# A decoder layer on one core: four per-layer-embedding products between the MLP's last sums, in source order

## The chip, the cores and the metric

The kernel runs on one core of one Trainium2 chip. The metric is the device time of one execution in microseconds (us), lower is better. Before the change three runs gave 1787.39, 1788.55 and 1790.4 us, so the median is 1788.55 us.

## The reference

One hybrid decoder layer over 1024 tokens of width 1024, all in float32: a dilated attention and an RWKV-7 time mix side by side, merged by gates, then a squared-ReLU MLP with 4096 hidden units, then a gated per-layer input embedding ("ple"). The change touches the last two parts:

```python
        f = rmsnorm(h, ffn_pre_norm[i])
        f = jnp.square(jax.nn.relu(f @ w_ff_in[i])) @ w_ff_out[i]
        h = h + rmsnorm(f, ffn_post_norm[i])
        e = (p[i] @ w_ple[i]) * jax.nn.sigmoid(h @ w_ple_gate[i])
        h = h + rmsnorm(e, ple_post_norm[i])
```

`p @ w_ple` (256 to 1024 columns) does not depend on `h`. `h @ w_ple_gate` does, and needs the MLP's output complete for its tokens.

## The kernel before, in words

**How a product is made.** Float32 products are made of three passes over halves that TensorE takes at full rate: every operand is split into a high part (ScalarE copies it, rounded) and a low part (VectorE or GpSimd subtracts the high part), and `mm3` issues high x high, high x low and low x high for each 128 rows of the contraction. The lines L291, L293 and L295 are these three. All elementwise instructions are recorded at one line, L116, all DMA requests at L133 (the SP queue), transposes at L282.

**Stages.** Input projections with the RWKV chain beside them (to about 470 us), attention (to about 830), merges and the output projection, first MLP matrix and second MLP matrix interleaved (about 1000 to 1626). The second matrix is multiplied by a seven-product scheme over 16 groups of 256 hidden units; its sums stand in SBUF tiles `tot`. The last group is multiplied plainly: `ff2_last(i, c)` computes, for token tile `i` (128 tokens, 8 of them) and column half `c`, six matmuls of 512 columns, and VectorE adds the PSUM bank to the sum `acc(i, c)`. The banks of these products rotate over three tags (`bank()`: s1, s2, s3), so a product waits until the bank used three products earlier has been read.

**After the sums.** `finish(i)` is a chain spawned after `ff2_last(i, 1)`: two squares with a row sum on ScalarE, a sum, a root and a reciprocal, two VectorE products with the gain row `g3`, two additions of the residual `hl` (loaded from `h_scr`, 256 KB per half, one buffer per half; the second addition on GpSimd for `i > 0`). Then `put_T` transposes the tile on TensorE and splits it (ScalarE `wh`, VectorE `wl`). `gate_mm(i)` multiplies it with `w_ple_gate` (48 matmuls) and takes the sigmoid into `sg`; `e_mm(i)` computes `p @ w_ple` for the tile (12 matmuls in two banks), multiplies by `sg`, squares, normalises, adds the tile and stores it. `last_weights` loads and splits the eight 128-row pieces of `w_ple_gate` (512 KB each, "wpg": two ScalarE copies and two GpSimd subtractions each) through the two buffers of raw rows `wr`; `ple_weights` does it for `p` and `w_ple` ("pq", four pieces) at the first `gate_mm`.

**What sets the order.** A planner (`Order`) runs over the program with its own costs: chains (`spawn`) go first when their time has come, dense products fill TensorE between them, and the order in which it emits instructions is the order of TensorE's queue everywhere. For the other four queues this order is binding only inside `tc.manual_schedule`; that is so from the RWKV stage until `attention` leaves it (L968). From there to the end the framework's scheduler orders VectorE, ScalarE, GpSimd and SP by its own rules, and may move later loads and splits ahead. The planner's cost of a VectorE instruction (`Engine`, L95 to L100) gets a factor of 1.25 when it has two tensor operands outside PSUM and `shared` is set; `attention` clears `shared`.

Of the kernel before, what the change touches and what calls it, by code (L numbers as in the profile page):

```python
# [18 lines left out]
D = 1024  # L19
# [18 lines left out]
LEAD, SPARE, LAG = 0.4, 0.5, 0.4  # L38
TABLE = {AF.Exp: 0, AF.Sqrt: 1, AF.Sigmoid: 2, AF.Tanh: 2}
# [18 lines left out]


def in_psum(x):  # L60
    return "PSUM" in type(x.tensor if hasattr(x, "tensor") else x[:].tensor).__name__.upper()
# [20 lines left out]
class Engine:  # L82
# [8 lines left out]
    def __getattr__(self, name):  # L91
        f = getattr(self.eng, name)

        def call(*a, **kw):
            n = max(math.prod(x.shape[1:]) for x in a if hasattr(x, "shape"))  # L95
            o = self.order
            us = self.fixed + n * self.per * (1.8 if name == "transpose" else 1.0)
            if self.shared and sum(hasattr(x, "shape") and math.prod(x.shape[1:]) > 1 and not in_psum(x)
                                   for x in (*a[1:], *kw.values())) > 1:
                us *= 1.25  # L100
            if name == "activation" and a[2] in TABLE and self.table != TABLE[a[2]]:
                us += 1.3
# [12 lines left out]
            o.dep = max(self.end, o.dep)  # L115
            return f(*a, **kw)  # L116
# [128 lines left out]
def layer(ctx: ExitStack, tc: tile.TileContext, x, pT, wz, wup, w_out, wff1, w_ff2, w_ple, w_pleg,  # L245
# [901 lines left out]
    def combine(OT, OA, stat, sel):  # L1147
# [56 lines left out]
    in_turn = tc.manual_schedule(  # L1204
        engines={mybir.EngineType.DVE, mybir.EngineType.Activation, mybir.EngineType.Pool, mybir.EngineType.SP})
# [333 lines left out]
    def ff1(j):  # L1539
        def body(hi, lo):  # L1540
# [58 lines left out]
    def ff2_last(i, c):  # L1599
        def body():  # L1600
# [5 lines left out]
            if i + c == 0:  # L1606
                last_weights()
# [5 lines left out]

    def last_weights():
# [11 lines left out]
    def ple_weights():  # L1626
        pq = pieces(("BK", "UV", "BK2", "r", "k"), "pq", F32R)
        P["p"], P["w"] = (pq[0:2], pq[2:4]), (pq[4:6], pq[6:8])
        P["sg"] = [rtile([128, D], "sg", t) for t in ("Ep", "En", "a", "kk")]
        t = rtile([128, 2, D], "eg", "BT")  # L1630
        P["eg"] = [rtile([128, D], "eg", "px"), t[:, 0], t[:, 1]]
        P["g4"] = rtile([128, D], "g4", "MP")
        SY.dma_start(P["g4"], gains[4:5, :].to_broadcast([128, D]))
        for k in range(2):
            wsplit(pT[k * 128:(k + 1) * 128, :], [(P["p"][0][k], P["p"][1][k], full)])
            wsplit(w_ple[k * 128:(k + 1) * 128, :], [(P["w"][0][k], P["w"][1][k], full)])

    hT = {}

    def finish(i):  # L1640
        yield from wait(lambda: i == 0 or i - 1 in hT and (i < 2 or ("G", i - 2) in done))
        a = [acc(i, 0), acc(i, 1)]
        r = ss2(a, [rtile([128, 512], "j", "gst") for c in range(2)])
        for c in range(2):
            hl = rtile([128, 512], "hl", ("ex", "py")[c])
            SY.dma_start(hl, h_scr[i][:, halves[c]])
            V.scalar_tensor_tensor(a[c], a[c], r, P["g3"][:, halves[c]], op0=OP.mult, op1=OP.mult)
            (G if c and i else V).tensor_tensor(a[c], a[c], hl, OP.add)
        yield sch.until(sch.dep + 0.3)
        hi = wpool.tile([128, KT, 128], F32R, name="wh")  # L1650
# [4 lines left out]
    def gate_mm(i):  # L1655
        def body():
            if i == 0:
                ple_weights()
# [11 lines left out]
        sch.add(body, None, lambda: i in hT and sch.t >= hT[i][2])  # L1670

    def e_mm(i):
        def body():
            ts = slice(i * 128, i * 128 + 128)
            sg, eg = P["sg"][i % 4], P["eg"][i % 3]
            cols = halves if i < 7 else (halves[0], slice(512, 768), slice(768, 1024))
            sc = small.tile([128, 4], F32, name="sc")
            for n, c in enumerate(cols):
                ps = bank()[:, 0:c.stop - c.start]
                yield from mm3(ps, [(P["p"][0][k][:, ts], P["p"][1][k][:, ts], P["w"][0][k][:, c],  # L1680
                                     P["w"][1][k][:, c]) for k in range(2)])
                V.tensor_tensor(sg[:, c], sg[:, c], ps, OP.mult)
                S.activation(ps, sg[:, c], AF.Square, accum_out=sc[:, n:n + 1])
                (V if n else G).tensor_tensor(eg[:, c], sg[:, c], P["g4"][:, c], OP.mult)
                if n:
                    V.tensor_tensor(sc[:, n:n + 1], sc[:, n - 1:n], sc[:, n:n + 1], OP.add)
            r = rstd_of(sc[:, n:n + 1], "rs")
            for c in cols:
                V.scalar_tensor_tensor(sg[:, c], eg[:, c], r,
                                       acc(i, c.start // 512)[:, c.start % 512:(c.stop - 1) % 512 + 1], op0=OP.mult, op1=OP.add)  # L1690
                SY.dma_start(out[i * 128:(i + 1) * 128, c], sg[:, c])
        sch.add(body, None, lambda: ("G", i) in done)
# [8 lines left out]
    for i in range(8):  # L1701
        for c in range(2):
            ff2_last(i, c)
    for i in range(8):
# [6 lines left out]
    sch.run()  # L1711

# [105 lines left out]
```

## Time and profile before

| | |
|---|---|
| median of three runs | 1788.55 us (1787.39 to 1790.4) |
| the profiled execution | 1786.45 us, its span 1784.7 us |
| TensorE busy (modelled ends) | 1751.1 us, 98% |
| VectorE, ScalarE, GpSimd busy | 1052.5, 728.2, 773.6 us |
| chain that ended last | TensorE 89%, VectorE 5%, ScalarE 3% |

The span is the time between the first and the last instruction seen; the execution's time is 1.75 us longer. A matmul of 512 columns is shown with a duration of 0.39 us, but the next starts 0.227 us later: they are pipelined, and what counts is the distance between starts. A number in brackets at the end of a row of the timeline is the idle time of the engine before it and what ended it.

### The profile page before, as it was taken

How to read it: one execution, taken by the hardware profiler on the slowest of the kernel's cores; microseconds unless marked ns; L12 is line 12 of the kernel's file. 1: busy time of each engine (PE TensorE's matmuls, PEld its weight loads, DVE VectorE, ACT ScalarE, POOL GpSimd, SP SyncE). 2: the span in 40 equal slices, each digit the busy share in tenths (PEclk: the TensorE clock that was granted, in tenths of full speed). 3: DMA queues.
4: the chain of work that ended last, by engine and by line, in shares of the span. 5: the costliest groups of instructions: out<-in, count | busy, mean ns of one | idle time of the engine just before them, and what ended most of it. 6: DMA issues, size and time to landing. Idle time of an engine off the chain costs nothing.

```text
span 1784.7 us, 25836 instructions
## 1 busy us (share of the span) xinstructions
PE 1751.1 (98%) x10192; PEld 1430.9 (80%) x10192; DVE 1052.5 (59%) x1866; ACT 728.2 (41%) x1301; POOL 773.6 (43%) x507
## 2 busy tenths in 40 slices
PE   9999989999999999999999999999999999999898
PEld 8787877878877877778888888888888888887786
DVE  6289777766535233353736565655655677888454
ACT  5824433332334343542524533333333333334353
POOL 1344131231232323332230366666666897986411
PEclk9999999999999999999999999999999999999999
DMA  4621121212242222333534211121111111113221
GB/s 161 210 95 37 48 77 42 90 42 95 84 146 77 66 60 71 100 120 133 200 95 142 83 60 59 50 69 48 48 48 48 53 54 48 48 48 100 93 79 48
DMA packets 51546, 146.13 MB, mean 82 GB/s; under 512 B 6241, under 2 KB 6625, under 8 KB 51426
## 3 DMA queue, kind: packets, MB, share of 16 engines
q1 hardware_dynamic: 51426, 144.49, 24.7%
q8 instruction: 80, 1.31, 0.3%
q14 instruction: 40, 0.33, 0.1%
HBM read 110.52 MB, written 27.26 MB: 77 GB/s over the span
## 4 chain that ended last, share of the span: by engine, by line
PE 89%; DVE 5%; ACT 3%; issue 2%; POOL 1%; DMA 0%; DVEq 0%; ACTq 0%; POOLq 0%
PE z L293 19%; PE z L295 19%; PE z L291 19%; PE bk L291 7%; PE bk L295 7%; PE bk L293 7%; DVE tot L116 1%; PE sc L274 1%; PE tp L282 1%; DVE xy L116 1%; PE A L274 1%; PE y L274 1%; PE po L274 1%; PE pt L282 1%; PE wr L274 1%
## 5 line engine op out<-in xcount | busy, mean ns | idle before, releaser
L116 DVE TENSOR_TENSOR tot<-tot,bk 128x512 f32<-128x512 f32 x468 | 308.1, 684 | 188.1 <-PE bk L295 187.4
L116 POOL TENSOR_TENSOR wl<-wr,wh 128x1024 fp32r<-128x1024 f32 (+1 forms) x87 | 211.5, 2431 | 442.2 <-ACT wh L116 423.0
L291 PE MATMUL z<-uh,wh 128*128 128x512 f32 (+1 forms) x800 | 313.6, 392 | 5.8 <-ACT part L116 3.0
L295 PE MATMUL z<-uh,wl 128*128 128x512 f32 (+1 forms) x800 | 314.2, 393 | 2.6 <-POOL wl L116 2.6
L293 PE MATMUL z<-ul,wh 128*128 128x512 f32 (+1 forms) x800 | 315.0, 394 | 0.3 <-DVE ul L116 0.3
L293 PE MATMUL z<-f,wh 128*128 128x512 f32 x496 | 193.1, 389 | 0.2 <-DVE f L116 0.2
L291 PE MATMUL z<-f,wh 128*128 128x512 f32 x496 | 193.2, 389 | 0.1
L295 PE MATMUL z<-f,wl 128*128 128x512 f32 x496 | 193.0, 389 | 0.0
L291 PEld LDWEIGHTS z<-uh,wh 128*128 128x128 f32 x800 | 152.0, 190 | 36.9 <-ACT part L116 3.5
L116 ACT ACTIVATE duo<-sum 128x512 fp32r<-128x512 f32 x150 | 90.3, 625 | 222.2 <-PE bk L295 117.1
L295 PEld LDWEIGHTS z<-uh,wl 128*128 128x128 f32 x800 | 152.0, 190 | 34.2 <-POOL wl L116 4.0
L293 PEld LDWEIGHTS z<-ul,wh 128*128 128x128 f32 x800 | 151.9, 190 | 31.0 <-issue 3.6
L291 PE MATMUL bk<-duo 128*128 128x512 f32 x420 | 163.4, 389 | 0.0
L295 PE MATMUL bk<-duo 128*128 128x512 f32 x420 | 163.4, 389 | 0.0
L293 PE MATMUL bk<-duo 128*128 128x512 f32 x420 | 163.4, 389 | 0.0
L116 POOL TENSOR_TENSOR duo<-sum,duo 128x512 fp32r<-128x512 f32 x75 | 101.1, 1348 | 98.6 <-ACT duo L116 95.8
L116 ACT ACTIVATE wh<-wr 128x1024 fp32r<-128x1024 f32 (+1 forms) x87 | 90.3, 1038 | 115.0 <-PE z L293 82.7
L116 POOL TENSOR_TENSOR sum<-w2r 128x512 f32<-128x512 f32 x75 | 98.8, 1318 | 64.1 <-DMA w2r<-in_w_ff_dram 59.3
L293 PEld LDWEIGHTS z<-f,wh 128*128 128x128 f32 x496 | 93.1, 188 | 19.8 <-DVE f L116 0.5
L291 PEld LDWEIGHTS z<-f,wh 128*128 128x128 f32 x496 | 93.1, 188 | 19.7 <-ACT f L116 0.4
L295 PEld LDWEIGHTS z<-f,wl 128*128 128x128 f32 x496 | 93.1, 188 | 19.3
L116 POOL TENSOR_TENSOR sum<-hr 128x512 f32<-128x512 f32 x75 | 97.6, 1310 | 4.8 <-DVE duo L116 3.1
(310 smaller groups left out, 3217.1 us busy)
## 6 DMA issues: line engine op xcount, KB each, us to landing
wr<-in_wz_dram SPq DMA_DIRECT2D x48, 512.0 KB, 3.9
w2r<-in_w_ff_dram SPq DMA_DIRECT2D x32, 512.0 KB, 3.5
wr<-in_wff_dram SPq DMA_DIRECT2D x31, 512.0 KB, 3.5
xt<-in_x_dram SPq DMA_DIRECT2D x16, 512.0 KB, 4.2
gscr<-gst SPq DMA_DIRECT2D x32, 256.0 KB, 2.1
g<-gscr SPq DMA_DIRECT2D x16, 512.0 KB, 4.2
sw<-qk SPq DMA_DIRECT2D x48, 128.0 KB, 2.3
sascr<-lst SPq DMA_DIRECT2D x16, 256.0 KB, 3.7
```

Of the source, the lines that this page charges most:

```text
L116: return f(*a, **kw)
L274: PE.matmul(out_, a, b, start=start, stop=stop)
L282: PE.transpose(out_, a, ident if idn is None else idn)
L291: PE.matmul(ps, ah, bh, start=i == 0, stop=False)
L293: PE.matmul(ps, ah, bl, start=False, stop=False)
L295: PE.matmul(ps, al, bh, start=False, stop=i == n - 1)
```

## The change

1. From the first `ff2_last` on, all queues run in source order: `manual_schedule` is entered again (`last["turn"]`), left after the run. The planner's engine times are cut back to at most 0.5 us ahead, and its record of writes starts anew.
2. `e_ahead(i)` for tiles 0 to 3: the 12 matmuls of `p @ w_ple` stand between the sums of tile `i` and tile `i + 1`, evacuated by ScalarE into `eg`; `e_mm(i)` of these tiles has no matmuls left.
3. The rows of `w_ple_gate` are requested by a chain (`loads`) when the planner holds a buffer free: four at once at the first `ff2_last` (two of them in the tile `UV`, which holds the last hidden activations), the rest one by one. GpSimd does all low parts. The chain marks "wpg" done; `gate_mm` waits for that in the planner.
4. The splits of `w_ple` and of half of `p` move into the last second-matrix products (after products 93, 97 and 101 of 0 to 104); the other half of `p` follows the gate's rows.
5. `finish` requests `hl` first, waits in the planner for its landing (not for tile 0), and marks ("H", i) after the additions; the next `finish` starts from there, no longer from the transposes. `put_T` waits for the buffers as before.
6. In the last tile the products with the gain `g4` follow the three squares, and the row sums are added at the end.
7. `in_psum` is gone: the factor of 1.25 holds for any two tensor operands while `shared` is set.

```diff
-            if self.shared and sum(hasattr(x, "shape") and math.prod(x.shape[1:]) > 1 and not in_psum(x)
+            if self.shared and sum(hasattr(x, "shape") and math.prod(x.shape[1:]) > 1
...
                         yield from product(n)
+                        if n in E_LOADS:
+                            e_weights(E_LOADS.index(n))
...
             if i + c == 0:
+                last["turn"] = tc.manual_schedule(engines=OTHERS)
+                last["turn"].__enter__()
+                sch.written = Written()
+                for e in (V, S, G, SY):
+                    e.end = min(e.end, sch.t + 0.5)
                 last_weights()
...
+    def loads(items, room=()):
+        flying = []
+        bufs = [(t, 0.0) for t in room] + [(None, 0.0)] * 2
+        items = list(items)
+        while items or flying:
+            if items and bufs and bufs[0][1] <= sch.t:
+                (src, two, split), (raw, _) = items.pop(0), bufs.pop(0)
+                if raw is None:
+                    raw = wpool.tile([128, 1024], F32, name="wr")
+                raw = k2(raw) if two else raw
+                flying.append((SY.dma_start(raw, src) + 0.3, split, raw))
+            elif flying and flying[0][0] <= sch.t:
+                _, split, raw = flying.pop(0)
+                split(raw)
+                bufs.append((None, G.end))
+            else:
+                t = [x[0] for x in flying[:1]] + [x[1] for x in bufs[:1] if items]
+                yield max(min(t) - sch.t, 0.0) + 0.05
...
-        for k in range(KT):
-            wsplit(w_pleg[k * 128:(k + 1) * 128, :],
-                   [(wpg[0][c][:, k, slice(0, 512)], wpg[1][c][:, k, slice(0, 512)], halves[c])
-                    for c in range(2)], eng2=G)
...
+        def chain():
+            yield from loads([(w_pleg[k * 128:(k + 1) * 128, :], None,
+                               halved([(wpg[0][c][:, k, slice(0, 512)], wpg[1][c][:, k, slice(0, 512)], halves[c])
+                                       for c in range(2)], G)) for k in range(KT)],
+                             pieces(("UV",), "wr", F32))
+            done.add("wpg")
+            yield from loads(e_weights(3))
+        sch.spawn(chain(), 2)
...
+    def e_ahead(i):
+        def body():
...
+            for c in halves:
+                ps = bank()
+                yield from mm3(ps, e_operands(i, c))
+                S.activation(P["eg"][i][:, c], ps, AF.Copy)
+        sch.add(body)
+
+    E_LOADS = (7 * NP - 19, 7 * NP - 15, 7 * NP - 11)
...
     def finish(i):
-        yield from wait(lambda: i == 0 or i - 1 in hT and (i < 2 or ("G", i - 2) in done))
+        yield from wait(lambda: i == 0 or ("H", i - 1) in done)
         a = [acc(i, 0), acc(i, 1)]
+        hl = [rtile([128, 512], "hl", ("ex", "py")[c]) for c in range(2)]
+        land = [SY.dma_start(hl[c], h_scr[i][:, halves[c]]) for c in range(2)][1]
+        yield sch.until(land if i else sch.dep)
         r = ss2(a, [rtile([128, 512], "j", "gst") for c in range(2)])
         for c in range(2):
-            hl = rtile([128, 512], "hl", ("ex", "py")[c])
-            SY.dma_start(hl, h_scr[i][:, halves[c]])
             V.scalar_tensor_tensor(a[c], a[c], r, P["g3"][:, halves[c]], op0=OP.mult, op1=OP.mult)
-            (G if c and i else V).tensor_tensor(a[c], a[c], hl, OP.add)
+        for c in range(2):
+            (G if c and i else V).tensor_tensor(a[c], a[c], hl[c], OP.add)
+        done.add(("H", i))
         yield sch.until(sch.dep + 0.3)
+        yield from wait(lambda: i == 0 or i - 1 in hT and (i < 2 or ("G", i - 2) in done))
...
+                if i < 4:
+                    V.tensor_tensor(sg[:, c], sg[:, c], eg[:, c], OP.mult)
+                    junk = rtile([128, 512], "j", "gst")
+                else:
+                    junk = bank()[:, 0:c.stop - c.start]
+                    yield from mm3(junk, e_operands(i, c))
+                    V.tensor_tensor(sg[:, c], sg[:, c], junk, OP.mult)
+                S.activation(junk, sg[:, c], AF.Square, accum_out=sc[:, n:n + 1])
+                if n == 0 or i < 7:
+                    (V if n else G).tensor_tensor(eg[:, c], sg[:, c], P["g4"][:, c], OP.mult)
+            for c in cols[1:] if i == 7 else ():
+                V.tensor_tensor(eg[:, c], sg[:, c], P["g4"][:, c], OP.mult)
+            for n in range(1, len(cols)):
+                V.tensor_tensor(sc[:, n:n + 1], sc[:, n - 1:n], sc[:, n:n + 1], OP.add)
...
             ff2_last(i, c)
+        if i < 4:
+            e_ahead(i)
```

## Rows read from the trace of the kernel before

**Rows 1.** Busy time by stretch: us, PE, PEld, DVE, ACT, POOL, PEclk, DMA share, GB/s
```profile
1640.00:1660.00 20.00, 14.51 (x58) 11.14 (x58) 18.05 (x26) 9.48 (x20) 17.28 (x11) 0.91 0.65 200
```

**Rows 2.** Timeline of TensorE, 1615 to 1665 us: start, us, what, idle before
```profile
1615.12 0.39 PE L291 MATMUL bk<-duo 128*128 128x512 f32 x1
...
1620.56 0.39 PE L291 MATMUL bk<-duo 128*128 128x512 f32 x1
...
1626.11 0.39 PE L291 MATMUL bk<-lw,lh 128*128 128x512 f32 x1
...
1640.94 0.79 PE L291 MATMUL bk<-lw,lh 128*128 128x512 f32 x1 [3.79 <-DVE tot L116]
...
1644.08 0.40 PE L293 MATMUL bk<-lwl,lh 128*128 128x512 f32 x1
...
1653.08 0.50 PE L291 MATMUL bk<-lw,lh 128*128 128x512 f32 x1 [0.90 <-DVE tot L116]
...
1654.58 1.03 PE L282 MATMUL tp<-cs,tot 128*128 128x128 f32 x8
1657.07 0.50 PE L291 MATMUL z<-wpg,wh 128*128 128x512 f32 x1 [1.46 <-ACT wh L116]
...
1660.89 0.63 PE L295 MATMUL z<-wpg,wl 128*128 128x512 f32 x1 [3.09 <-DVE wl L116]
...
1664.65 0.39 PE L295 MATMUL z<-wpg,wl 128*128 128x512 f32 x1
```

**Rows 3.** Timeline of VectorE around the stalls, and one undisturbed pair later
```profile
1634.57 3.45 DVE L116 SCALAR_TENSOR_TENSOR tot<-tot,rs,g 128x512 f32<-128x512 f32 x2
1637.94 2.35 DVE L116 TENSOR_TENSOR tot<-tot,hl 128x512 f32<-128x512 f32 x2
1640.21 1.87 DVE L116 TENSOR_TENSOR tot<-tot,bk 128x512 f32<-128x512 f32 x3
...
1663.21 1.86 DVE L116 TENSOR_TENSOR tot<-tot,hl 128x512 f32<-128x512 f32 x1 [1.78 <-DMA hl<-hscr]
...
1698.22 1.42 DVE L116 SCALAR_TENSOR_TENSOR tot<-tot,rs,g 128x512 f32<-128x512 f32 x2
```

**Rows 4.** Timeline of GpSimd: the last split that a product waits for
```profile
1611.77 1.30 POOL L116 TENSOR_TENSOR duo<-sum,duo 128x512 fp32r<-128x512 f32 x1 [2.82 <-issue]
```

**Rows 5.** Timeline of SP's queue: start, us, requests
```profile
1605.18 7.01 SPq L133 DMA_DIRECT2D hl<-hscr  x2
1628.83 10.66 SPq L133 DMA_DIRECT2D wr<-in_w_pleg_dram  x4
```

**Rows 6.** Tile hl (256 KB each, 16 of them): from request to landing
```profile
DMA to landing us min/median/max: 2.5/2.9/5.3
```

**Rows 7.** Tile xt (512 KB, eight requests of 1.2 to 7.0 us): request and landing
```profile
L133 SPq DMA_DIRECT2D xt<-in_x_dram x8: 327/430/650, 1.2 to 7.0; - x8
...
DMA to landing us min/median/max: 3.5/8.3/10.2
```

**Rows 8.** Tile wpg: splits of the gate's rows, ns min/median/max
```profile
L116 POOL TENSOR_TENSOR wpg<-wr,wpg x16: 1279/1378/1857, 1616.5 to 1653.5; 128x512 fp32r<-128x512 f32 x16
```

**Rows 9.** Tile j: squares of the finished sums on ScalarE, ns min/median/max
```profile
L116 ACT ACTIVATE j<-tot x16: 615/617/632, 1628.9 to 1732.8; 128x512 f32<-128x512 f32 x16
```

**Rows 10.** Timeline of VectorE in the last tile
```profile
1777.36 1.21 DVE L116 TENSOR_TENSOR eg<-sg,g 128x256 f32<-128x256 f32 x1
1778.50 0.41 DVE L116 TENSOR_TENSOR sg<-sg,bk 128x256 f32<-128x256 f32 x1
...
1779.48 0.16 DVE L116 TENSOR_TENSOR sc<-sc 128x1 f32<-128x1 f32 x1
...
1780.27 1.54 DVE L116 SCALAR_TENSOR_TENSOR sg<-eg,rs,tot 128x512 f32<-128x512 f32 x3
```

**Rows 11.** Waits of TensorE, 100 to 560 us: us in total, times, longest
```profile
PE z L291 <- ACT part L116: 3.0, 1, 3.0
```

**Rows 12.** VectorE by form, 100 to 500 us: the costliest with a PSUM operand
```profile
L116 DVE TENSOR_TENSOR TM<-A,cs 128x512 f32<-128x512 f32 x32 | 20.4, 682 | 12.0 <-PE A L274 11.9
```

More of the change, by code (lines that the diff above doesn't have):

```diff
@@ L57, in place @@
     return x.tensor.name, (p, p + n, f, f + 1 + sum((k - 1) * s for s, k in free))
-def in_psum(x):
-    return "PSUM" in type(x.tensor if hasattr(x, "tensor") else x[:].tensor).__name__.upper()
 class Written:
@@ L1612, in layer, with halved, split, e_weights @@
     P = {}
+    def loads(items, room=()):
[16 more added lines that the diff above has]
+                yield max(min(t) - sch.t, 0.0) + 0.05
+    def halved(outs, eng):
+        def split(raw):
+            for hi, lo, sl in outs:
+                S.activation(hi, raw if sl is None else raw[:, sl], AF.Copy)
+                eng.tensor_tensor(lo, raw if sl is None else raw[:, sl], hi, OP.subtract)
+        return split
+    def e_weights(n):
+        if n < 2:
+            hi, lo = pieces((("AR1",), ("AR0",))[n], "pq", F32R)
+            for x, t in zip(P.setdefault("w", ([], [])), (hi, lo)):
+                x.append(t)
+            wsplit(w_ple[n * 128:(n + 1) * 128, :], [(hi, lo, full)])
+            return
+        h = n - 2
+        p = [k2(x) for x in pieces((("BT",), ("UV",))[h], "pp", F32R)]
+        P[f"p{h}"] = p
+        src = pT[:, halves[h]].rearrange("(k p) c -> p k c", p=128)
+        if h == 0:
+            wsplit(src, [(p[0], p[1], None)], 2)
+        return [(src, 2, halved([(p[0], p[1], None)], G))]
     def last_weights():
@@ L1632, in ple_weights, with ple_tiles, e_operands @@
+        sch.spawn(chain(), 2)
+    def ple_tiles():
+        t = rtile([128, 2, D], "sg", "BK")
+        P["sg"] = [rtile([128, D], "sg", t) for t in ("Ep", "En", "kk")] + [t[:, 0]]
         P["g4"] = rtile([128, D], "g4", "MP")
         SY.dma_start(P["g4"], gains[4:5, :].to_broadcast([128, D]))
-        for k in range(2):
-            wsplit(pT[k * 128:(k + 1) * 128, :], [(P["p"][0][k], P["p"][1][k], full)])
-            wsplit(w_ple[k * 128:(k + 1) * 128, :], [(P["w"][0][k], P["w"][1][k], full)])
+    def e_operands(i, c):
+        h, ts = tok(i)
+        p = P[f"p{h}"]
+        return [(p[0][:, k, ts], p[1][:, k, ts], P["w"][0][k][:, c], P["w"][1][k][:, c]) for k in range(2)]
@@ L1638, in layer @@
+    def e_ahead(i):
+        def body():
+            if i == 0:
+                t = rtile([128, 2, D], "eg", "BK2")
+                P["eg"] = [t[:, 0], t[:, 1]] + [rtile([128, D], "eg", t) for t in ("a", "px")]
+            for c in halves:
[4 more added lines that the diff above has]
+    E_LOADS = (7 * NP - 19, 7 * NP - 15, 7 * NP - 11)
     hT = {}
     def finish(i):
-        yield from wait(lambda: i == 0 or i - 1 in hT and (i < 2 or ("G", i - 2) in done))
+        yield from wait(lambda: i == 0 or ("H", i - 1) in done)
@@ L1669, in body @@
             done.add(("G", i))
-        sch.add(body, None, lambda: i in hT and sch.t >= hT[i][2])
+        sch.add(body, None, lambda: "wpg" in done and i in hT and sch.t >= hT[i][2])
     def e_mm(i):
         def body():
-            ts = slice(i * 128, i * 128 + 128)
-            sg, eg = P["sg"][i % 4], P["eg"][i % 3]
+            sg, eg = P["sg"][i % 4], P["eg"][i % 4]
             cols = halves if i < 7 else (halves[0], slice(512, 768), slice(768, 1024))
@@ L1678, in body @@
             for n, c in enumerate(cols):
[L1679 to L1686, printed above, removed]
+                if i < 4:
[12 more added lines that the diff above has]
+                V.tensor_tensor(sc[:, n:n + 1], sc[:, n - 1:n], sc[:, n:n + 1], OP.add)
             r = rstd_of(sc[:, n:n + 1], "rs")
@@ L1711, in layer @@
     sch.run()
+    last["turn"].__exit__(None, None, None)
 _INS = ["x", "pT", "wz", "wup", "w_out", "wff1", "w_ff2", "w_ple", "w_pleg", "lora", "prm", "gains",
```

14 lines of the change are left out of this document (5 added, 9 removed).

## The prediction

> **What bounds the kernel now.** I read the page first: TensorE is busy for 98% of the span, so a change elsewhere pays only where TensorE stands. Busy time by stretch then shows where that is near the change: from 1640 to 1660 us TensorE falls to 14.51 of 20 us while VectorE is at 18.05 and GpSimd at 17.28 [rows 1]. TensorE's timeline of that stretch names the stalls: 3.79, 0.90, 1.46 and 3.09 us, all ended by VectorE or ScalarE [rows 2]. VectorE's own timeline says why: at 1634.57 it goes into `finish(0)`, two products with the gain row for 3.45 us and two additions for 2.35 us, and only then reads the PSUM banks that TensorE wants back [rows 3]. The same pair takes 1.42 us at 1698, when GpSimd is idle. So this stretch is bound by VectorE's queue, lengthened by GpSimd's splits beside it.
>
> What can be won is countable. A bracket counts from a modelled end 0.39 us after a start, while starts come 0.227 us apart (24 matmuls in the 5.44 us from 1615.12 to 1620.56), so each stall costs 0.16 more: 9.24 + 4 x 0.16 = 9.9. After the first and the last stall the matmuls run at the lower clock, 1.2 of 2.4 GHz by their distance of 0.43: seven in 3.14 us and nine in 3.76 instead of 1.59 and 2.04, another 3.3. Together 13.2 us lost before 1664.65 [rows 2]. From there to the last tile the timeline shows TensorE without a stall.
>
> **The change, part by part.**
>
> *Moved products.* Four times 12 matmuls go from the gate stage to the sums: 48 x 0.227 = 10.9 us taken there and added here, no change in the sum. Its worth is time for VectorE: tiles 0 to 3 last 24 matmuls, 5.44 us, instead of 2.72, and half of their banks are read by ScalarE.
>
> *Earlier splits.* Three GpSimd subtractions of 128x1024, twice the 128x512 form, about 3 x 2.6 us [rows 8], and three ScalarE copies enter the second-matrix stage; two gate pieces that the scheduler now puts there leave it. The last split for a product ends at 1613.07 [rows 4] and its matmuls start at 1620.56 [rows 2]: 7.5 us cover one such insertion. I take 0. Without that cover each costs up to 2.6 us.
>
> *SP's order: the residual now stands behind the gate's rows.* Today `hl` of tile 0 was requested at 1605, long before the sums [rows 5]. In source order SP issues after the first sum: four pieces of 512 KB, the first two only when the tile `UV` is free, then the two `hl` halves. Today's first request of this stretch is at 1628.83 [rows 5]; about then the last hidden half has been split, so I take 1629.1 and steps of 0.4. A single 512 KB load lands in 3.5 us. The queued ones: the last of eight x tiles, requested at 7.0, lands after 10.2 us, at 17.2, some 12.5 us after the first, with two weight tiles among them and a constants tile of half the size, that is 1.3 us for each [rows 7]. So the four land at about 1632.6, 1633.9, 1635.2 and 1636.5, the `hl` halves at 1637.1 and 1637.8. Bounds, from the request of the second half at 1631.1: a lone `hl`'s 2.5 us [rows 6], 1633.6; the longest queued load's 10.2 us [rows 7], 1641.3, which would lengthen the stall below by 3.5.
>
> The Trainium skill (DMA: Bandwidth & Descriptors, Queues, rings and completion order) says that on each DMA engine the descriptors of one issuing queue are consumed in ring order. By that the residual lands last, as in my sum; the eight x tiles agree, growing from 3.5 to 10.2 us. By the lone `hl`'s row the sum would be rival A's.
>
> *First stall.* `finish(0)` puts all its VectorE instructions into the queue at once, ahead of the sums of tile 1. Its products run early and undisturbed, but the additions stand for `hl`. TensorE meanwhile has seven products of 1.36 us, to 1626.11 + 9.52 = 1635.6; the eighth needs the bank of tile 1's first sum, and the transposes of tile 0 need the additions. Additions beside GpSimd 1.17 each [rows 3]: 1639.5; the sum 0.6: 1640.2. TensorE goes on at 1640.3 instead of 1636.4 (0.8 for eight transposes in between, 1.03 with a modelled end [rows 2]): 3.9 lost, and at the lower clock 0.6 to 1.5 more. I take 4.5.
>
> *Tiles 1 to 3: a line of waits.* In source order ScalarE reaches the squares of tile i only after its copy of the bank before, and VectorE does nothing past a `finish` until ScalarE has answered. One turn is: copy 0.6 and two squares 0.62 each with a readout [rows 9], 2.0 with the hops; sum, root, reciprocal to the first product 0.8 (1779.48 to 1780.27 [rows 10]); two products 1.4 alone to 3.4 beside GpSimd, addition 0.6 to 1.2, next sum 0.6 [rows 3]; then the product whose bank this frees, 1.36. That is 6.8 to 9.4 against 5.44 of TensorE per tile. GpSimd itself waits for `finish` between pieces, so I take 7.2: 1.8 lost per turn, three turns, 5.4. Behind them tile 4's `finish` stands ahead of tile 6's sum: 1.0. Both ends: 0 to 4.0 per turn; nothing if VectorE is never behind, since the turns cover each other only while the planner's distances hold.
>
> *Gate rows.* 16 subtractions of 1.38 [rows 8], 22 us, start near 1633.3; with `finish`'s additions (1.3 each) among them and two waits for buffers they end around 1662. The sums end at 1626.1 + 34.2 (24 products of 1.36, two sets of transposes) + 10.9 lost = 1671. Hidden. By the same cover the 0.4 us requests for `g4` and the other half of `p` cost nothing; were it gone, `gate_mm(0)` would stand for each piece 2.8 us.
>
> *Sum for this stretch:* 4.5 + 5.4 + 1.0 = 10.9 lost instead of 13.2: 2.3 won.
>
> *Last tile.* VectorE takes the last product with the sigmoid at 1778.50, behind a gain product of 1.21 us; with the products first, only that gain product and the smaller one follow. The two row sums then end 0.2 to 0.3 earlier than 1779.64 [rows 10]. I take 0.2; bounds 0 and 0.8.
>
> *`in_psum`.* Only the RWKV stage has `shared` set. There the planner's price of 128x512 with PSUM rises from 0.71 to 0.89; the trace has 0.682 [rows 12]. TensorE's order shifts by fractions of a microsecond, filled with gate projections, which last beyond attention. I take 0. The longest wait there is 3.0, and not for VectorE [rows 11]; one more or one fewer such wait with its stretch at the lower clock bounds a reshuffled order by about 4 us either way.
>
> **Sum.** 2.3 + 0.2 = 2.5 us less than the profiled 1786.45: 1783.95. The median stands 2.1 us above that execution, so for a median 1788.55 - 2.5 = 1786.05, call it 1786. A measurement of this kernel can tell about 0.2%, 3.6 us, from no change.
>
> **Rivals.**
>
> A, *the residual is in time.* If the `hl` halves land by 1635 (a lone one's 2.5 to 2.9 us), VectorE is never behind, the planner's distances of 5.44 us hold, and only the turns of tiles 3 and 4, emitted before sums that follow 2.72 us apart, cost 1.4 each: 2.8 lost. 13.2 - 2.8 + 0.2 = 10.6 won, 1778. For it: request and landing of lone halves. Against: 2 MB ahead in the same queue. Chance 0.22.
>
> B, *the lines feed each other, slower.* The place is VectorE's queue at every `finish`. From stalls of about 3 us on TensorE comes back at the lower clock (1.6 us lost after the 3.79 stall and 1.7 after 3.09, none to speak of after 0.90 [rows 2]). If the turns take 8.4, each stands 3 us and pays the clock too: 5.5 + 3 x (3.0 + 1.6) + 1.0 = 20.3 lost, 7 us slower, 1795.5; it decides from a turn of 7.7 on, where the loss passes 13.2. For it: `finish`'s products at 3.45 a pair. Against: GpSimd waits too, so pairs at 1.4. The Trainium skill (TensorE: Matmul & The Clock Gate, the table of specifications) calls the queues of VectorE, ScalarE and GpSimd strict FIFO: the addition that stood 1.78 us for `hl` [rows 3] held all behind it, as the rule has it. Chance 0.17.
>
> C, *the RWKV stage decides.* Its reshuffle moves more than the tail: 4 us either way, 1782 or 1790. Against: nothing there stands on VectorE for long. Chance 0.11, half each side.
>
> The forecast, 10.9 lost with an own range of 8 to 14: 1783 to 1789.5. Chance 0.50.
>
> **How the numbers follow.** Faster by over 0.2% (below 1785): A, half of C and 0.28 of the forecast's range: 0.22 + 0.05 + 0.14 = 0.41. Slower (above 1792): most of B and some of C, 0.16. The same: 0.43. The range that holds 8 in 10 takes most of A and the near part of B: 1777.5 to 1792.5.
>
> **What would show it.** First step: `hl` requested after the gate's pieces, VectorE's first addition standing for `hl` until about 1637, a TensorE stall of about 4 us with matmuls 0.43 apart behind it. Turns: stalls of about 2 us before the second `bk<-pq` of tiles 2 and 3 and in tile 5's sums, ended by VectorE `tot`. Gate rows: no wait for `wpg`. Splits: no stall before 1626. The prediction is wrong if TensorE passes 1635 to 1640 without a stall (A), if several stretches run at the lower clock (B), or if TensorE reaches the first sum more than 2 us away from 1626.1 (C).

## The result, and the profile after

The changed kernel takes 1792.36 us (median of 19 runs, 1787.66 to 1796.8), the kernel before 1788.55 in the same count: ratio 1.0022, 95% interval 1.0013 to 1.0031, slower by 2.3 to 5.5 us. The profiled execution's span is 1789.0 us against 1784.7. Three marks on TensorE's timeline cut both spans into four parts: the first product of the second matrix (`bk<-duo`), the first of the last sums (`bk<-lw,lh`), the last matmul of the last product (`bk<-pq`, after the change `bk<-pq,pp`).

| part of the span | before | after | difference | forecast |
|---|---|---|---|---|
| start to first `bk<-duo` | 1022.16 | 1019.98 | -2.18 | 0 |
| to the first sum | 603.95 | 610.29 | +6.34 | 0 |
| to the last product | 151.13 | 151.74 | +0.61 | -2.3 |
| to the end | 7.46 | 6.99 | -0.47 | -0.2 |

The first row is spread between executions, not the change: in fourteen profiles the first `bk<-duo` starts between 1019.7 and 1027.8 us. Up to there the kernels before and after show the same instructions in the same order, by tile names (without buffer numbers) and shapes, on all five engines (6882 records of TensorE, 1147 of VectorE), and so do experiments 1 and 4, which start it at 1024.35 and 1020.07. The second row is the loss.

TensorE's timeline after, 1019 to 1682 us (columns as in [rows 2], with which the second half compares):
```profile
1019.98 0.39 PE L288 MATMUL bk<-duo 128*128 128x512 f32 x1
...
1562.27 0.50 PE L288 MATMUL bk<-duo 128*128 128x512 f32 x1 [0.17 <-DVE tot L113]
...
1571.14 0.51 PE L288 MATMUL bk<-duo 128*128 128x512 f32 x1 [0.23 <-DVE tot L113]
...
1617.35 0.51 PE L288 MATMUL bk<-duo 128*128 128x512 f32 x1 [0.23 <-DVE tot L113]
...
1624.34 0.50 PE L288 MATMUL bk<-duo 128*128 128x512 f32 x1 [1.42 <-DVE tot L113]
...
1630.27 0.39 PE L288 MATMUL bk<-lw,lh 128*128 128x512 f32 x1
...
1646.57 0.80 PE L288 MATMUL bk<-pq,pp 128*128 128x512 f32 x1 [6.62 <-DVE tot L113]
1647.16 1.91 PE L279 MATMUL tp<-cs,tot 128*128 128x128 f32 x8
...
1652.71 0.44 PE L290 MATMUL bk<-lwl,lh 128*128 128x512 f32 x1
...
1656.48 0.50 PE L288 MATMUL bk<-pq,pp 128*128 128x512 f32 x1 [0.36 <-DVE tot L113]
...
1665.62 0.50 PE L288 MATMUL bk<-lw,lh 128*128 128x512 f32 x1 [1.12 <-DVE tot L113]
...
1673.16 0.50 PE L288 MATMUL bk<-lw,lh 128*128 128x512 f32 x1 [1.51 <-DVE tot L113]
...
1678.73 0.39 PE L288 MATMUL z<-wpg,wh 128*128 128x512 f32 x1
```
Two clusters of waits for VectorE stand ahead of 1630, where the kernel before has none. Set product against product from the first `bk<-duo`, TensorE falls back 2.60 us between 1562 and 1571.2 and 3.71 from 1617 to 1627; elsewhere in these 600 us the two keep step within about 0.1. The clusters are several waits of about 0.2, each with the 0.16 of a modelled end and a matmul of 0.5, so the brackets alone would not have shown their size.

What VectorE did there (its timeline after: one line ahead of the first cluster, the two clusters, and the start of the sums):
```profile
1545.50 1.10 DVE L113 TENSOR_TENSOR duo<-sum,duo 128x512 fp32r<-128x512 f32 x1 [5.12 <-ACT duo L113]
...
1558.50 2.52 DVE L113 TENSOR_TENSOR duo<-hr,duo 128x512 fp32r<-128x512 f32 x1 [0.93 <-ACT duo L113]
1560.94 4.86 DVE L113 TENSOR_TENSOR tot<-tot,bk 128x512 f32<-128x512 f32 x8
...
1612.95 1.95 DVE L113 TENSOR_TENSOR duo<-sum,duo 128x512 fp32r<-128x512 f32 x1 [2.00 <-ACT duo L113]
1614.83 4.86 DVE L113 TENSOR_TENSOR tot<-tot,bk 128x512 f32<-128x512 f32 x8
1619.61 3.48 DVE L113 TENSOR_TENSOR lhl<-hr,lh 128x512 fp32r<-128x512 f32 x2
1623.02 4.86 DVE L113 TENSOR_TENSOR tot<-tot,bk 128x512 f32<-128x512 f32 x8
...
1635.39 1.42 DVE L113 SCALAR_TENSOR_TENSOR tot<-tot,rs,g 128x512 f32<-128x512 f32 x2
1642.53 3.39 DVE L113 TENSOR_TENSOR tot<-tot,hl 128x512 f32<-128x512 f32 x2 [5.73 <-DMA hl<-hscr]
1645.84 1.27 DVE L113 TENSOR_TENSOR tot<-tot,bk 128x512 f32<-128x512 f32 x2
```
The same places before:
```profile
1545.40 1.10 DVE L116 TENSOR_TENSOR duo<-sum,duo 128x512 fp32r<-128x512 f32 x1 [2.83 <-ACT duo L116]
...
1557.41 1.16 DVE L116 TENSOR_TENSOR duo<-hr,duo 128x512 fp32r<-128x512 f32 x1
1558.88 4.87 DVE L116 TENSOR_TENSOR tot<-tot,bk 128x512 f32<-128x512 f32 x8 [0.31 <-PE bk L295]
...
1611.14 0.69 DVE L116 TENSOR_TENSOR duo<-sum,duo 128x512 fp32r<-128x512 f32 x1 [1.15 <-ACT duo L116]
1611.75 4.86 DVE L116 TENSOR_TENSOR tot<-tot,bk 128x512 f32<-128x512 f32 x8
1616.54 2.39 DVE L116 TENSOR_TENSOR lhl<-hr,lh 128x512 fp32r<-128x512 f32 x2
```
GpSimd's timeline after, beside it:
```profile
1558.07 2.40 POOL L113 TENSOR_TENSOR pq<-wr,pq 128x1024 fp32r<-128x1024 f32 x1
...
1611.96 2.40 POOL L113 TENSOR_TENSOR pp<-wr,pp 128x1024 fp32r<-128x1024 f32 x1 [2.01 <-ACT pp L113]
1614.31 1.76 POOL L113 TENSOR_TENSOR duo<-sum,duo 128x512 fp32r<-128x512 f32 x1
...
1619.59 2.95 POOL L113 TENSOR_TENSOR lwl<-w2r,lw 128x1024 fp32r<-128x1024 f32 x1 [1.18 <-PE bk L292]
```
and ScalarE's:
```profile
1556.88 1.06 ACT L113 ACTIVATE pq<-wr 128x1024 fp32r<-128x1024 f32 x1 [1.90 <-POOL tot L113]
1557.85 0.61 ACT L113 ACTIVATE duo<-hr 128x512 fp32r<-128x512 f32 x1
...
1610.84 1.04 ACT L113 ACTIVATE pp<-wr 128x1024 fp32r<-128x1024 f32 x1
...
1612.30 1.14 ACT L113 ACTIVATE duo<-sum 128x512 fp32r<-128x512 f32 x2
```
Each costly split works twice. Its copy on ScalarE (1.06 and 1.04 us) stands ahead of the copies for `duo`, so VectorE's `duo` begins late; and its subtraction on GpSimd runs beside that `duo`, which then takes 2.52 us instead of 1.16 in the first cluster and 1.95 instead of 0.69 in the second. In the second cluster the `lhl` pair adds to it: now it runs beside GpSimd's `lwl` and takes 3.48 instead of 2.39. Eight additions take 4.86 with GpSimd busy (1614.83) and with GpSimd idle (from 1623.02 on, `lwl` having ended at 1622.54). From start to start, a short `duo` and eight additions are 5.40 us (1611.14 to 1616.54 before), TensorE's product 5.44: what VectorE loses here it does not win back.

The first of the three splits costs TensorE nothing, but it is not free. Counted from the first `bk<-duo`, VectorE's `duo` behind it begins 2.28 us later than before (1545.50 and 1545.40), since GpSimd spends 2.87 us on the split at 1532.75 and hands on everything behind it later. This lateness still stands when the second split comes: the eight additions of 1560.94 begin 4.24 us later than before, of which TensorE loses 2.60. Of these 4.24 some 2.25 are from the first split, 1.0 is the copy and 1.4 the longer `duo`, less 0.4 that VectorE had spent waiting before.

SP's queue after, and the answer for tile `hl` ([rows 5, 6] before): the four gate rows go first, and the slowest `hl` half lands after 7.6 us.
```profile
1633.15 1.75 SPq L130 DMA_DIRECT2D wr<-in_w_pleg_dram  x4
1634.95 11.32 SPq L130 DMA_DIRECT2D hl<-hscr  x4
```
```profile
DMA to landing us min/median/max: 2.6/2.8/7.6
```
Busy time by stretch after (columns and the first stretch before: [rows 1]): from 1640 to 1660 TensorE loses more, although VectorE is half as busy.
```profile
1640.00:1660.00 20.00, 13.07 (x47) 10.50 (x48) 9.97 (x14) 10.24 (x23) 12.97 (x11) 0.74 0.40 130
1660.00:1680.00 20.00, 17.36 (x78) 13.49 (x77) 15.55 (x27) 10.09 (x24) 14.32 (x10) 1.00 0.46 135
```

### The profile page after: what moved, and what is told of

Same layout as the page of the kernel before. It is cut to its first block, busy times and chain, and to the rows that moved or that the text cites. A ratio compares the mean times of both kernels' runs of the same rounds, so it can differ in the third digit from the quotient of the medians.

```text
span 1789.0 us, 25850 instructions
## 1 busy us (share of the span) xinstructions
PE 1751.5 (98%) x10192; PEld 1428.1 (80%) x10192; DVE 1056.9 (59%) x1866; ACT 734.9 (41%) x1311; POOL 771.6 (43%) x507
```

## The experiments

Each was timed beside the kernel before on one chip, in sets on four chips (1 to 4, 5 to 8, 9 to 11, 12). "Distance" is from the first `bk<-duo` to the first sum, and from there to the last product, in the profile of each.

| kernel | ratio, 95% interval | to the first sum | to the last product |
|---|---|---|---|
| before | 1 | 603.95 | 151.13 |
| changed | 1.0022 (1.0013, 1.0031) | 610.29 | 151.74 |
| 1 splits moved | 1.0015 (1.0002, 1.0028) | 608.71 | 150.66 |
| 2 `hl` first | 1.0023 (1.0012, 1.0035) | 610.35 | 149.59 |
| 3 `in_psum` back | 1.0039 (1.0024, 1.0053) | 610.37 | 151.65 |
| 4 = 1 and 2 | 1.0001 (0.9988, 1.0013) | 607.99 | 148.83 |
| 5 `pp` behind `lwl` | 1.0000 (0.9988, 1.0013) | 606.85 | 151.60 |
| 6 chain later | 1.0002 (0.9989, 1.0015) | 610.33 | 146.99 |
| 7 rows ahead | 0.9993 (0.9979, 1.0006) | 607.97 | 148.36 |
| 8 before, new price | 1.0002 (0.9989, 1.0015) | 603.96 | 153.17 |
| 9 `lwl` behind `lhl` | 1.0004 (0.9993, 1.0015) | 604.74 | 151.65 |
| 10 six banks | 1.0006 (0.9992, 1.0019) | 611.47 | 148.33 |
| 11 all | 0.9969 (0.9958, 0.9979) | 604.68 | 145.73 |
| 12 `hl` a tile ahead | 0.9967 (0.9955, 0.9979) | 604.68 | 146.15 |

The first number repeats within 0.1 us between kernels of the same order there (610.29, 610.35, 610.37, 610.33), with one exception: in 1, 7 and 10 five to seven matmuls behind the second cluster came 0.43 us apart instead of 0.227, which adds 0.72, 1.12 and 1.2 us against 4, 5 and the changed kernel. A step of 2 us is a finding. The second is less steady: before and 8 run the same instructions in the same order, yet differ by 2.0, with the granted clock at 0.91 in one and 0.83 in the other from 1640 to 1680.

**1: the splits at other places.**
```diff
+        if n + 2 == 7 * NP - 12:
+            with tc.issue_after(S.ins), tc.issue_after(V.ins):
+                e_weights(1, V)
...
                             last_split(0, (0, 1), (0,))
+                            with tc.issue_after(last["duo"]), tc.issue_after(G.ins):
+                                e_weights(2)
```
(`S.ins`, `V.ins`, `G.ins` are the instructions issued last on these engines, so the split's place in the queue is set. `e_weights(1, V)` also moves that subtraction from GpSimd to VectorE. The first split stays where it was.)

> The changed kernel with two of its three early splits of ple moved inside the second-matrix stage. The split of the second half of w_ple goes into VectorE's pause behind product 98 (its subtraction on VectorE), the split of p's first half behind the last products' copies on ScalarE and behind the first lwl subtraction on GpSimd. Theory S (place): the two splits cost TensorE 2.60 us at product 94 and 3.71 us from product 103 on, because ScalarE's 1.06 us copy stands ahead of the copies for duo and GpSimd's 2.40 us subtraction runs beside VectorE's duo, which then takes 1.95 to 2.52 instead of 0.69 to 1.16. Elsewhere they cost nothing: the first lw sum starts at about 1624 us instead of 1630.3, and the time falls by 6.3 us, 0.9987 of the kernel before. Rival W (work): VectorE and GpSimd are full there, and the same work costs the same anywhere: no change, 1.002 of the kernel before. Rival L (given back): TensorE comes earlier to the sums, but hl is requested as late as before, so the stall behind it grows by what was won: span unchanged.

A part of it came: 1.58 of 6.34 us by the distance, 2.30 in experiment 4, which has the same splits and no matmuls at 0.43 there; the ratio alone tells nothing. The 2.60 us at product 94 are gone: TensorE waits for nothing ahead of 1620. The other split cost as much as before, by another contact (VectorE's timeline, then GpSimd's):
```profile
1620.58 4.60 DVE L113 TENSOR_TENSOR lhl<-hr,lh 128x512 fp32r<-128x512 f32 x2
```
```profile
1619.43 2.41 POOL L113 TENSOR_TENSOR pp<-wr,pp 128x1024 fp32r<-128x1024 f32 x1
1621.80 2.83 POOL L113 TENSOR_TENSOR lwl<-w2r,lw 128x1024 fp32r<-128x1024 f32 x1
```
The `lhl` pair reads both its operands from SBUF, as `duo` does, and now stands between two long GpSimd subtractions. The split at product 94 fits theory S and not W; for the other the place was wrong.

**2: `hl` of tile 0 requested first.**
```diff
             if i + c == 0:
+                hl_load(0)
                 last["turn"] = tc.manual_schedule(engines=OTHERS)
```
(`hl_load(i)`, whose definition is left out here, requests both halves of tile `i`.)

> The changed kernel with the two hl halves of tile 0 requested ahead of the source-ordered part, so ahead of the gate's four rows. Theory H: the 6.62 us stall before the sums of tile 1 and the matmuls at 0.43 us behind it come from hl alone; VectorE's additions then start right behind the gain products, about 1637 instead of 1642.5, and 5 to 8 us go: 1784 to 1787 us, 0.997 to 0.999 of the kernel before. Rival V (VectorE's queue is the bound): the products and additions of finish(0), now beside GpSimd's splits, take 3.4 and 2.4 us as in the kernel before, the stall shrinks only to about 4 us or comes back at the next tiles, and less than 3 us go: 1.0005 or more.

A miss in time, and instructive. The additions do come right behind the gain products, at 1639.88, 1.29 us the pair, and TensorE passes the old place of the stall. 6.3 us on it stands again. The three lines are from VectorE's, ScalarE's and TensorE's timelines:
```profile
1645.95 1.29 DVE L113 TENSOR_TENSOR wl<-tp,wh 128x512 fp32r<-128x512 f32 x2 [3.47 <-ACT wh L113]
```
```profile
1640.01 4.93 ACT L113 ACTIVATE wpg<-wr 128x512 fp32r<-128x512 f32 x8 [0.34 <-DMA wr<-in_w_pleg_dram]
```
```profile
1653.31 0.80 PE L288 MATMUL bk<-pq,pp 128*128 128x512 f32 x1 [3.86 <-DVE tot L113]
```
ScalarE does eight copies of gate rows ahead of the copy `wh` of tile 0's transposes, and VectorE, in source order, stands for `wh` with the next sums behind it. The rival's size came, by another engine than it named.

**3: `in_psum` put back.**
```diff
-            if self.shared and sum(hasattr(x, "shape") and math.prod(x.shape[1:]) > 1
+            if self.shared and sum(hasattr(x, "shape") and math.prod(x.shape[1:]) > 1 and not in_psum(x)
```

> The changed kernel with in_psum put back, so the planner's old price for VectorE's reads of PSUM in the RWKV stage. Theory P: the 2.2 us by which the changed kernel leads at 1020 us come from that price alone; the first bk product starts at 1022.2 instead of 1020.0 and the time rises by 2.2 us, 1.0034 of the kernel before. Rival N: the lead is an accident of one execution (or of other orders), and nothing moves: 1.0022.

Rival N. The time is 0.17% above the changed kernel's, with intervals that overlap, but the two are the same program: on all five engines the instructions come in the same order over the whole span, by tile names and shapes (10192 records of TensorE, 1866 of VectorE). The higher time is not the price's work.

**4: both.**

> The first two together: splits moved, hl of tile 0 requested first. If theories S and H both hold and their terms add, 6.3 and 5 to 8 us go from the changed kernel: 1778 to 1781 us, 0.994 to 0.996 of the kernel before. If VectorE's queue at the sums is the bound (rival V), only the splits' 6.3 and under 3 us go: 0.997 to 0.9987.

1.0001, above both ranges: what both had won, no more. Their gains add (769.02 us from the first `bk<-duo` to the end after, 766.45, 767.02 and here 763.83), but neither was whole.

**5: `pp` behind the second `lwl`** (against 1).
```diff
                             last_split(0, (0, 1), (0,))
-                            with tc.issue_after(last["duo"]), tc.issue_after(G.ins):
-                                e_weights(2)
...
                             last_split(1, (0,), (1,))
+                            with tc.issue_after(last["duo"]), tc.issue_after(G.ins):
+                                e_weights(2)
```

> The first experiment with one more step: the split of p's first half stands behind the second lwl subtraction on GpSimd, so beside VectorE's additions from PSUM and no longer beside its lhl subtractions. In the first experiment GpSimd went from pp straight into lwl, and VectorE's lhl pair beside them took 4.6 us (2.39 in the kernel before); TensorE stood 2.5 us for it. Theory S2 (a split costs by what VectorE does beside it: an instruction with both operands in SBUF is stretched, an addition from PSUM is not): the lhl pair takes 1.3 to 2.4 us, the 2.5 us stall goes, and the first lw sum comes 604.0 to 604.6 us after the first bk product (603.95 in the kernel before, 610.3 in the changed one, 608.7 in the first experiment): 4 us less than the first experiment, 0.999 of the kernel before. Rival W: VectorE is simply full before the sums, the stall moves to another product, and the distance stays above 607.5: 1.001 or more.

Between the two: 606.85. The pair took 3.49, since now `lwl` itself, freed of `pp`, began with it (VectorE's timeline, then GpSimd's):
```profile
1615.91 3.49 DVE L113 TENSOR_TENSOR lhl<-hr,lh 128x512 fp32r<-128x512 f32 x2
```
```profile
1615.91 2.93 POOL L113 TENSOR_TENSOR lwl<-w2r,lw 128x1024 fp32r<-128x1024 f32 x1 [1.10 <-PE bk L293]
```

**6: the chain of gate rows 6 us later** (on top of 2).
```diff
-        sch.spawn(chain(), 2)
+        sch.spawn(chain(), 2, 6.0)
```

> The second experiment (hl of tile 0 first) with the chain of the gate's rows started 6 us later, so that ScalarE's copies of tile 0's transposes (wh) stand ahead of its eight copies of gate rows and no longer behind them. Theory A (ScalarE's queue): with hl in time the stall only moved 6.7 us on, because ScalarE did eight gate copies, waiting for their rows, ahead of wh, and VectorE stood 3.5 us for wh with the additions of the next sums behind it. Then the 3.86 us stall falls below 1.5 us and 3 to 5 us go: 1787 to 1789 us, 0.9995 to 1.001 of the kernel before. Rival V2: VectorE's own finish chain, or gate rows that now come late for the gate's matmuls, give the same loss at another place: 1.002 as before.

The 3.86 us stall is gone, and one of 5.53 has come a tile later: the burst of gate copies, six now, stood ahead of the squares of tile 1 instead of `wh` (TensorE's timeline, then ScalarE's):
```profile
1653.04 0.79 PE L288 MATMUL bk<-lw,lh 128*128 128x512 f32 x1 [5.53 <-DVE tot L113]
```
```profile
1642.60 3.22 ACT L113 ACTIVATE wpg<-wr 128x512 fp32r<-128x512 f32 x6
```
Theory A holds for the place, and 1.0002 lies in its range. But the two stalls of this stretch are as long together as in 2 (5.53 and 1.65 against 3.86 and 3.47), which is V2; the distance is 2.6 us shorter because 5 matmuls came 0.43 apart here and 17 in 2.

**7: corrections together (2, 5 and 6), two gate rows ahead of the sums** (`last_gate(n)` requests and splits `n` rows; left out here).
```diff
+                last_gate(2)
                 last["turn"] = tc.manual_schedule(engines=OTHERS)
```

> All corrections together: splits of ple at the places of the last experiment but one, hl of tile 0 first, the chain of gate rows 6 us later, and two of the eight gate rows split ahead of the sums, where GpSimd stands idle for 15 us. If theories S2, H and A hold and add, the first lw sum comes at 604.3 us after the first bk product and the sums lose under 6 us instead of 13.8: 1777 to 1782 us, 0.9935 to 0.9965 of the kernel before. If VectorE's queue at the sums is the bound: 0.997 to 0.999.

Neither range: 0.9993, with the same stall, 5.54 us, behind six copies. The first sum came after 607.97 us and not 604.3, since 5's place for the split was not yet the right one.

**8: the kernel before with the new price.**

> The kernel before with in_psum alone taken out, nothing else. Theory P: the planner's new price shortens the RWKV stage by 2 to 2.7 us: 0.9985 to 0.9989 of the kernel before. Rival N: the lead of 2.2 us in the profile is the spread between executions (the first bk product starts at 1019.98, 1020.07, 1023.08 and 1024.35 in four profiles of the same early program): 1.000.

No change, rival N. Here too the order of instructions is the same on all five engines over the whole span, as it was in 3: the price of PSUM reads moved no instruction. So 3 and 8 are repeats of the changed kernel and of the one before, and show how far one program spreads: 0.17% in the ratio, 2.0 us in the second distance.

**9: `lwl` waits for the `lhl` pair** (on top of 5).
```diff
+            if k:
+                tc.add_manual_dep(G.ins, last["lhl"].name, mybir.DependencyInfo(
+                    mybir.DependencyClass.Sync, mybir.DependencyReason.DATA))
```

> The third placing of p's split with one step more: GpSimd's second lwl subtraction waits for VectorE's lhl pair (in that run it began at 1615.91 with the pair, which took 3.49 us, and TensorE then stood 1.38 us and three times 0.23 for VectorE). Theory S2 (what counts is whether VectorE's instruction beside a GpSimd split has both operands in SBUF): the lhl pair takes about 1.3 us, no stall for VectorE is left before the first lw sum, which comes 603.9 to 604.4 us after the first bk product (606.85 in that run); about 2.7 us go, and TensorE reaches the sums as early as in the kernel before although GpSimd and ScalarE do the three splits more. Rival W (VectorE full): the distance stays above 606.

VectorE's timeline, then GpSimd's:
```profile
1616.13 1.29 DVE L113 TENSOR_TENSOR lhl<-hr,lh 128x512 fp32r<-128x512 f32 x2
```
```profile
1617.55 2.42 POOL L113 TENSOR_TENSOR lwl<-w2r,lw 128x1024 fp32r<-128x1024 f32 x1 [2.51 <-issue]
1619.92 2.39 POOL L113 TENSOR_TENSOR pp<-wr,pp 128x1024 fp32r<-128x1024 f32 x1
```
The pair takes 1.29 and the distance is 604.74, 0.3 over the range but 5.55 of the 6.34 us back, with every split still done ahead of the sums (one of the subtractions on VectorE). Only `lwl` has moved since 5, and with it the pair's time and the distance: theory S2 is shown, W is refuted. The ratio (1.0004) agrees with the distance only in direction: it is 0.0018 below the changed kernel, 3 us, with intervals that overlap by 0.0002.

**10: six banks for the sums** (on the changed kernel).
```diff
-            ps = bank()
+            ps = bank(SIX if i < 6 else SIX[0:3])
...
-                ps = bank()
+                ps = bank(SIX)
```

> The changed kernel with six PSUM banks in place of three for the last sums of tiles 0 to 5 and the four ahead products, nothing else moved. Theory Q: TensorE stands at the sums because VectorE, in order, comes back late for the bank three products on, 4.1 us; VectorE's lateness does not add up from tile to tile. Then three more banks cover 4.1 us: the 6.62 us stall falls to about 2.5 us, the later ones of 0.4 to 1.5 us go, and TensorE needs about 144 us from the first lw sum to the last bk product instead of 151.7: 5 to 8 us less, 0.9985 to 1.000 of the kernel before. Rival V3: VectorE's work per tile is longer than TensorE's 5.4 us, so a wider cover only moves the stalls to the later tiles: the distance stays above 149 us.

3.4 us of distance, not 5 to 8, and not above 149 as V3 has it. The first stall stayed, now ahead of tile 0's transposes (4.13 and 1.02 us, for the additions of `hl`), which no bank helps; a later one of 1.98 came where three banks take over.

**11: all of it (2, 7, 9 and 10), gate rows one at a time,** the chain 2 us later in place of 6.
```diff
                 split(raw)
                 bufs.append((None, G.end))
+                yield 3.5
```

> All corrections together: splits of ple and the second lwl subtraction beside VectorE's additions from PSUM, hl of tile 0 first, two gate rows split ahead of the sums, the others one at a time (3.5 us between them) and no longer in bursts of eight copies on ScalarE, six PSUM banks for the sums. If the theories hold: first lw sum 604.2 us after the first bk product, 143 to 146 us from there to the last bk product (151.1 before, 151.7 in the changed kernel), together 6 to 9 us less than the kernel before: 0.995 to 0.9965. If VectorE's work per tile bounds the sums: 0.997 to 0.999.

0.9969, 0.9958 to 0.9979: faster than both kernels, by 5.5 us against the one before, a little short of the range. One long stall is left, and ahead of it VectorE's longest wait is `hl` again, of tile 2 (VectorE, then TensorE); experiment 12 asks whether the one makes the other:
```profile
1651.13 0.69 DVE L113 TENSOR_TENSOR tot<-tot,hl 128x512 f32<-128x512 f32 x1 [3.25 <-DMA hl<-hscr]
```
```profile
1662.45 0.79 PE L289 MATMUL bk<-lw,lh 128*128 128x512 f32 x1 [4.41 <-DVE tot L113]
```

**12: `hl` a tile ahead** (two more buffers for it).
```diff
+        hl, land = hls[i]
+        if i < 7:
+            hl_load(i + 1)
```

> The kernel with all corrections, and hl of every tile requested one tile ahead (two more 128x512 buffers), so ahead of the gate's rows on SP's queue. In the run with all corrections VectorE still stood 3.25 us for hl of tile 2 and 0.84 us for that of tile 3, and TensorE 4.41 us at 1662.45. Theory R (what stands behind 512 KB rows on SP's queue lands late, at each tile): no wait for hl is left on VectorE before 1665, the 4.41 us stall falls below 2 us, and TensorE needs 141 to 143.5 us from the first lw sum to the last bk product (145.7 in that run): 2 to 4 us less, 0.995 to 0.996 of the kernel before. Rival V4: VectorE and ScalarE are then full, the stall stays or comes as another turn: 0.9965 to 0.9975.

Rival V4. No wait for `hl` is left on VectorE, and yet TensorE stands 5.00 us: a stall of that size comes without it. VectorE's turns are 6.0 to 7.8 us long (`ss` at 1640.46, 1646.45, 1654.22, 1660.78) against TensorE's 5.4. From TensorE's timeline, and from the longest turn on VectorE's:
```profile
1665.40 0.80 PE L289 MATMUL bk<-lw,lh 128*128 128x512 f32 x1 [5.00 <-DVE tot L113]
```
```profile
1647.43 2.93 DVE L113 SCALAR_TENSOR_TENSOR tot<-tot,rs,g 128x512 f32<-128x512 f32 x2
```
The pair takes 1.41 us alone; beside the gate's splits it takes twice that. That this lengthening is what makes the stall is read from the trace; no run takes it out.

A reckoning over the 265 timed runs with a mean granted clock on record, one slope for that clock, leaves a scatter of 1.2 us and puts the changed kernel at +5.9 us against the kernel before (0.6 either way), 9 at +1.2, 11 at -3.3 and 12 at -3.4 (0.7 to 0.8). It is a check on the order only: a stall lowers the mean clock too, and so part of an effect is taken out with it.

## Why the prediction was wrong

**The step that failed is "Earlier splits: I take 0".** It measured 6.3 us: 2.60 and 3.71 with the second and third split, none with the first, which only used up VectorE's slack. The prediction named up to 2.6 each "without that cover". The cover was read from GpSimd's queue alone: last subtraction at 1613.07, matmuls at 1620.56 [rows 4, 2]. The path to those matmuls' successors goes through ScalarE's copy, VectorE's `duo` and VectorE's additions, and VectorE had little slack there (of 4.24 us TensorE lost 2.60). The prediction had the contact in its own rows, `finish`'s pair at 3.45 us beside GpSimd and 1.42 without [rows 3], and used it for the sums but not one stage earlier. Experiments 1, 5 and 9 show it: the same subtractions at other places, one of them on VectorE, and `lwl` behind the `lhl` pair cost 0.8 instead of 6.3. How much of the 6.3 is ScalarE's copy alone was not run; the starts above put it at about 1 us of VectorE's lateness for each split.

**First stall: right in kind, 4.5 forecast.** `hl` did go behind the gate's pieces and landed in 7.6 us against the 6.7 forecast from the second half's request. TensorE resumed 16.3 us after the first sum instead of 14.2: the landing, and additions at 3.39 the pair instead of 2.34 beside GpSimd. With the lower clock behind it (matmuls 0.43 apart until 1652.71: 6.1 us for ten matmuls and eight transposes, 2.3 at 0.227 and 0.8) it cost 6.8 + 3.1 = 9.9. Of rival A (the residual in time) experiments 2 and 4 show that its premise would not have given its 1778: the wait turns into ScalarE's queue of gate copies. That VectorE works in the order of its queue shows here better than in the row given for rival B, behind which nothing stood ready: the sums of 1645.84 waited behind the addition of 1642.53, though TensorE had issued the last of their matmuls before 1639.

**Turns: forecast 6.4, measured about 3.5** (0.36, 1.12 and 1.51, each 0.16 more). Standing for `hl` let GpSimd finish eight subtractions, so the later pairs ran at 1.41 to 1.87. First stall and turns together are 13.4, and by the marks 13.2 + 0.6 = 13.8 were lost where 10.9 was forecast; the 0.6 over the kernel before are less than the 2.0 by which two executions of the same work differ here. So the 2.3 us to be won at the sums did not show either: with the splits' loss taken back (experiment 9, 1.0004) the change is level with the kernel before, not faster.

**Right:** the moved products are neutral; no wait for `wpg` at 1678.73; the last tile gained 0.47 (forecast 0.2, bound 0.8); the planner's price is 0, since it changes the order of no instruction. The text's own sign of failure, the first sum more than 2 us away from 1626.1, came true at 1630.27, but by the splits and not by rival C's RWKV stage, whose order of instructions is unchanged. That 1792.36 lies just inside the stated 1777.5 to 1792.5 is luck: the upper end was kept open for B and C, and neither came. Rival B (lines that feed each other) did not come: no second stretch at the lower clock.

On the contact the Trainium skill (SBUF — State Buffer, Who interferes with whom) says that a VectorE instruction with two SBUF inputs contends with a GpSimd instruction that reads SBUF, one with at most one SBUF input does not, and that the shared ports are an exclusive lock. The trace agrees on all three: additions from PSUM take 4.86 in either case; the `lhl` pair takes 1.29 with GpSimd idle beside it (experiment 9) and 2.39, 3.49 and 4.60 beside GpSimd's subtractions (before, 5, 1); and the `duo` of 1558.50 and 1612.95 end at 1561.02 and 1614.90, 0.55 and 0.54 us behind the end of GpSimd's subtraction (1560.47, 1614.36), about as if they had only then begun.

## What to carry to other kernels

A step is hidden only if every engine on the way from it to the bound has slack: check the queue it joins, the copies it stands ahead of, and what runs beside it, not just the engine that does it. Where GpSimd must work under a VectorE that is full, put its instructions beside VectorE's reads of PSUM, and keep them away from instructions with two SBUF operands. Source order on all engines makes every early request, copy and split a possible wait for what is written behind it; a wait that is taken out (here `hl`) shows the next one in the same queues (`wh`, then the squares, then VectorE's own long turns), so correct them together before judging.

## What the runs showed of the hardware

- GpSimd pays for the contact too, but less: its 128x1024 subtraction takes 2.40 alone and 2.83 to 2.96 beside VectorE's `lhl` pair (2.83 in experiment 1, 2.96 in 7).
- Executions of one program differ mostly ahead of the second matrix: its first product started anywhere from 1019.7 to 1027.8 us, while the 600 us behind it repeat within 0.1 in kernels of the same order, or within 1.2 where a stretch at the lower clock comes in. A difference of 2 us in a whole span says little; the same 2 us between two marks of one stage say much.
- After a stall of 6.62 us TensorE's matmuls came 0.43 apart for 6.1 us, and the granted clock of that 20 us stretch was 0.74; after stalls of 1.12 and 1.51 the stretch from 1660 to 1680 has 1.00.
- Behind a shorter stall the lower clock comes in one execution and not in another of the same order up to there: matmuls 0.43 apart followed waits of 2.53 (experiment 1), 1.41 (7) and 1.46 us (10), but not those of 2.44 (4), 1.38 (5) and 1.42 (the changed kernel). In 10 the granted clock from 1633.4 to 1637 was 0.53.
